# A block inversion that keeps one product and asks for its transpose two steps later, score products on 64 rows, and one modulation sum per step

## The chip, the cores and the metric

The kernel runs on one core of a Trainium2 chip. The metric is the device time of one execution in microseconds, taken as the median of several executions. Below, PE is TensorE (matrix products into PSUM banks), DVE is VectorE, ACT is ScalarE, POOL is GpSimd, and SP issues most of the DMAs. All of them run their own instructions in order and wait for each other through semaphores.

## The reference, cut to what matters

The whole kernel is two network blocks over 256 tokens of width 1024. The change lies in one stage of the first block, an RWKV-7 state recurrence with 8 heads of 64 values, and in the modulation vector that is made beside it.

```python
mod = jax.nn.silu(c) @ cond_w + cond_b          # 6 x 1024 values, one weight column per value

def step(state, inp):                            # once per token and head
    r_t, w_t, k_t, v_t, kk_t, a_t = inp
    sa = jnp.einsum('bhvk,bhk->bhv', state, -kk_t)
    state = (state * w_t[:, :, None, :]
             + sa[..., None] * (kk_t * a_t)[:, :, None, :]
             + v_t[..., None] * k_t[:, :, None, :])
    y_t = jnp.einsum('bhvk,bhk->bhv', state, r_t)
    return state, y_t
_, ys = lax.scan(step, state0, xs)
```

## The kernel before

The kernel does not step through the tokens. It cuts the 256 tokens into two chunks of 128, so that with 8 heads there are 16 pairs of chunk and head, numbered `u`. Within a pair, the effect of the tokens on each other is a strictly triangular 128 x 128 matrix of scores, and the recurrence needs the inverse of one minus that matrix. Four pairs share a PSUM bank of 512 columns and form a group `g`.

**Scores.** `amat` multiplies 128 channels of keys with 256 columns of `AR`, for one pair at a time, and DVE masks the result to a triangle (`mskb`). Two heads lie on the 128 channels. `AR` holds zeros in the 64 rows of the other head, so that the product over all 128 rows gives one head's scores. `AB` holds the scores for the inversion and `AK` those for the values.

**Inversion.** It goes by levels of doubled block size, `li` from 0 to 6. `TT` holds the inverse so far and `TN` its transpose. POOL cuts the off-diagonal blocks of a level out of `AB` into `off` (`lv_off`, one of four buffers). Level 0 sets `TT` to `off` plus one and makes `TN` from a product of `off` with the identity (`lv0`). Each later level has two parts for each group: `lvW` multiplies `off` with `TN` and lets ACT move the result into `W`; `lvD` multiplies `TT` with `W` and adds that to `TN` on DVE, and multiplies `W` with `TT` and adds that to `TT` on DVE. The 24 pairs of level (1 to 6) and group are the steps `k` of the loop over `todo`; step `k` issues `lvW` of step `k + 1` and then `lvD` of step `k`. The last level, steps 20 to 23, changes only `TT`.

**Beside the loop.** After each step `next(sd)` issues one piece of side work: the `AK` scores (`amat`), transpositions to token order (`to_tok`, and those into `RH1`), and the products of `AK` with the values (`akv`). Those take two heads' value columns for each pair, and ACT keeps the half that belongs to the head. A modulation sum (`modblk`) loads 512 KB of `cond_w` into one of three `wraw` buffers, and DVE multiplies it with `c_row` and sums along the rows (L310). It writes its products, which nobody reads, into `junk`. 24 sums stand in this stage. At one step the layer norm of the convolution branch is issued too (column sums L292 and L304, then Ln, Exp and Silu on ACT, then `ychi` and `yclo`).

**Order.** The code gives the order in which work is written, and a scheduler places the instructions on the five engines from it. Semaphores follow from who writes and reads a buffer. The weights of the next stage (`w_out`) go through the same three `wraw` buffers behind the modulation weights, and are split on ACT (L201) and DVE (L202).

Of the kernel before, what the change touches and what calls it, by code (L numbers as in the profile page):

```python
# [15 lines left out]
AF = mybir.ActivationFunctionType  # L16
# [143 lines left out]
def body(ctx: ExitStack, tc: tile.TileContext, A: dict, out: bass.AP):  # L160
# [169 lines left out]
    with ExitStack() as c1:  # L330
# [258 lines left out]
        mskb = con("msk")[:, None, :].to_broadcast([P, 2, 256])  # L589

        def amat(src, dst, u0):
            ps = bank()
            for uu in range(2):
                u = u0 + uu
                tb, h = u // 8, u % 8
                pe.matmul(ps[:, uu * T : (uu + 1) * T], src[:, h // 2, tb * P : (tb + 1) * P], AR[:, h % 2, h // 2, tb].rearrange("p a t -> p (a t)"), start=True, stop=True)
            dve.tensor_tensor(dst[:, u0 : u0 + 2].rearrange("p u a t -> p u (a t)"), r3(ps, 2), mskb, op=OP.mult)


        TT = tl([P, 16, P], "TT", "X1")  # L600
# [14 lines left out]
        def lv0(g):  # L615
            off = offs[0, g]
            dve.tensor_tensor(TT[:, gsl(g)], off, idb, op=OP.add)
            ps = bank()
            for uu in range(4):
                pe.matmul(ps[:, uu * P : (uu + 1) * P], off[:, uu], ident, start=True, stop=True)  # L620
            dve.tensor_tensor(TN[:, gsl(g)], r3(ps, 4), idb, op=OP.add)

        def lvW(li, g):
# [8 lines left out]
        def lvD(li, g):  # L632
            if li < 6:
                ps2 = bank()
                for uu in range(4):
                    pe.matmul(ps2[:, uu * P : (uu + 1) * P], TT[:, g * 4 + uu], W[:, g * 4 + uu], start=True, stop=True)
                dve.tensor_tensor(TN[:, gsl(g)], TN[:, gsl(g)], r3(ps2, 4), op=OP.add)
            ps1 = bank()
            for uu in range(4):
                pe.matmul(ps1[:, uu * P : (uu + 1) * P], W[:, g * 4 + uu], TT[:, g * 4 + uu], start=True, stop=True)  # L640
            dve.tensor_tensor(TT[:, gsl(g)], TT[:, gsl(g)], r3(ps1, 4), op=OP.add)


        vN = tl([P, 2, 512], "vN")
# [10 lines left out]
        def akv(g):  # L655
            ps = bank()
            tb = g // 2
            for uu in range(4):
                u = g * 4 + uu
                hp = (u % 8) // 2  # L660
                pe.matmul(ps[:, uu * P : (uu + 1) * P], AK[:, u, 0], vN[:, tb, hp * P : (hp + 1) * P], start=True, stop=True)
            h0 = (g % 2) * 4
            for pr in range(2):
                src = ps.rearrange("p (h r n) -> p h r n", h=2, r=4)[:, :, 3 * pr]
                if tb == 0:
                    dst = RH0[:, h0 : h0 + 4].rearrange("p (h r) n -> p h r n", r=2)[:, :, pr]
                else:
                    dst = RH1[:, h0 : h0 + 4].rearrange("p (h r) x n -> p h r x n", r=2)[:, :, pr, 1]
                act.activation(dst, src, AF.Copy)

        def side():

            for u0 in range(0, 16, 2):
                amat(ktT, AK, u0)
                yield
            for tb in range(2):
# [15 lines left out]

        for u0 in range(0, 16, 4):
            amat(bT, AB, u0)
            amat(bT, AB, u0 + 2)
            lv_off(0, u0 // 4)
        sd = side()
        for g in range(4):
# [9 lines left out]
        for k, (li, g) in enumerate(todo):  # L708
            if k + 1 < len(todo):
                lvW(*todo[k + 1])  # L710
            lvD(li, g)
            next(sd, None)
            if k % 2:
                modblk(next(mrest), c_row, junk)
            if k == 10:

                xcc, sqc = tl([P, 4, T], "xcc", "vT"), tl([P, 4, T], "sqc", "ug")
                rstdc = layer_norm(pa, yc, xcc, sqc, 4, "conv")
                ychi, yclo = tl([P, 4, T], "ychi", "yc", F32R), tl([P, 4, T], "yclo", "ug", F32R)
                for b in range(4):  # L720
                    dve.tensor_tensor(xcc[:, b], xcc[:, b], rstdc, op=OP.mult)
                    act.activation(xcc[:, b], xcc[:, b], AF.Silu, scale=col("conv_ln_g", b), bias=col("conv_ln_b", b))
                    asplit(ychi[:, b], yclo[:, b], xcc[:, b])
# [9 lines left out]
        HG = tl([P, 16, 2, 64], "HG", "X4")  # L733
        for g in range(4):
            ps = bank()
            for uu in range(4):
                u = g * 4 + uu
                h = u % 8
                if g < 2:
                    rhs = RH0[:, h - h % 2 : h - h % 2 + 2].rearrange("p a n -> p (a n)")  # L740
                else:
                    rhs = RH1[:, h].rearrange("p a n -> p (a n)")
                pe.matmul(ps[:, uu * P : (uu + 1) * P], TT[:, u], rhs, start=True, stop=True)
            if g < 2:
                for pr in range(2):
                    src = ps.rearrange("p (h r n) -> p h r n", h=2, r=4)[:, :, 3 * pr]
                    act.activation(HG[:, g * 4 : g * 4 + 4].rearrange("p (h r) x n -> p h r x n", r=2)[:, :, pr, 1], src, AF.Copy)
            else:
                act.activation(HG[:, g * 4 : g * 4 + 4].rearrange("p u a n -> p u (a n)"), r3(ps, 4), AF.Copy)


        Sb = tl([P, 4, P], "Sb", "RH0")
# [730 lines left out]
```

## Time and profile before

| what | value |
|---|---|
| median of 3 executions | 1485.28 us (1483.69 to 1488.85) |
| profiled execution, its own time | 1487.35 us |
| span from first to last instruction in it | 1485.3 us |
| PE busy / DVE busy / ACT busy | 96% / 70% / 52% of the span |
| mean granted TensorE clock | 0.989 |

The stage of the change is the stretch from about 105 to 225 us of the span, 8% of it. A time below that names a moment counts from the start of the span. PE runs a float32 product as two passes, so the trace has two records for each product, and one record for a transposition.

### The profile page before, as it was taken

What the parts mean: (1) busy time and instruction counts of PE and PEld (TensorE: products, weight loads), DVE (VectorE), ACT (ScalarE), POOL (GpSimd) and SP (SyncE); (2) the same over time, 40 slices, a digit from 0 to 9 for tenths busy, and PEclk for the clock granted to TensorE, in tenths of its full rate; (3) what the DMA queues carried; (4) which work ended last, traced back from release to release, by engine and by line L of the source; (5) the groups of instructions that cost most, each with busy time, mean ns of one, the idle gap of its engine ahead of it and who ended that gap; (6) DMA issues with size and microseconds to landing.
All of it is one profiled execution on the core that took longest, in us unless ns stands there. A gap on an engine that the chain in (4) does not pass through costs nothing.

```text
span 1485.3 us, 26041 instructions
## 1 busy us (share of the span) xinstructions
PE 1427.0 (96%) x10380; PEld 1316.3 (89%) x10381; DVE 1039.1 (70%) x1895; ACT 769.0 (52%) x1210; POOL 137.5 (9%) x96
## 2 busy tenths in 40 slices
PE   9999899799899999999999999999998999899997
PEld 6887798799899999999988888888887989799997
DVE  7779846689946777778865566655556745598886
ACT  3731436845445555444455444544446555666554
POOL 0115310134440000000000000000001000000000
PEclk9999999999999999999999999999999999999998
DMA  9676403354455555555556677766662534265552
GB/s 384 207 201 196 146 30 102 92 163 156 142 185 171 166 161 167 162 169 168 160 184 195 201 227 227 218 205 190 194 189 93 169 100 144 84 187 190 189 188 85
DMA packets 71864, 252.09 MB, mean 170 GB/s; under 512 B 7982, under 2 KB 11967, under 8 KB 70848
## 3 DMA queue, kind: packets, MB, share of 16 engines
q1 hardware_dynamic: 68990, 245.40, 52.3%
q10 hardware_dynamic: 2754, 5.05, 1.0%
q8 instruction: 81, 1.33, 0.4%
q14 instruction: 39, 0.32, 0.1%
HBM read 248.25 MB, written 2.16 MB: 169 GB/s over the span
## 4 chain that ended last, share of the span: by engine, by line
PE 82%; DVE 10%; ACT 4%; issue 2%; DMA 1%; POOL 0%; DVEq 0%; SPq 0%; ACTq 0%; POOLq 0%
PE bk L1073 23%; PE bk L213 16%; PE bk L214 16%; PE bk L216 15%; DVE junk L310 3%; PE bk L292 1%; PE bk L1005 1%; PE bk L1006 1%; PE bk L304 1%; DMA wraw<-in_cond_dram 1%; DVE wlo L202 1%; DVE eq L967 1%; ACT whi L201 1%; PE bk L640 1%; PE bk L901 1%
## 5 line engine op out<-in xcount | busy, mean ns | idle before, releaser
L201 ACT ACTIVATE whi<-wraw 128x1024 fp32r<-128x1024 f32 x400 | 423.6, 1060 | 466.3 <-PE bk L214 240.2
L202 DVE TENSOR_TENSOR wlo<-wraw,whi 128x1024 fp32r<-128x1024 f32 x376 | 462.7, 1232 | 264.8 <-ACT whi L201 256.7
L213 PE MATMUL bk<-hhi,whi 128*128 128x256 f32 x1152 | 288.5, 288 | 0.0
L214 PE MATMUL bk<-hlo,whi 128*128 128x256 f32 x1152 | 285.7, 285 | 2.2 <-DVE hlo L277 2.2
L1073 PE MATMUL bk<-whi,zs 128*128 128x512 f32 x1024 | 253.3, 390 | 1.7 <-ACT zs L276 1.7
L1073 PEld LDWEIGHTS bk<-whi,zs 128*128 128x128 f32 x1024 | 191.9, 188 | 42.3 <-ACT zs L276 1.9
L214 PEld LDWEIGHTS bk<-hlo,whi 128*128 128x128 f32 x1152 | 222.7, 193 | 2.4 <-DVE hlo L277 2.4
L213 PEld LDWEIGHTS bk<-hhi,whi 128*128 128x128 f32 x1152 | 222.7, 193 | 0.0
L216 PE MATMUL bk<-hhi,wlo 128*128 128x256 f32 x1152 | 163.1, 285 | 7.2 <-DVE wlo L202 7.0
L216 PEld LDWEIGHTS bk<-hhi,wlo 128*128 128x128 f32 x1152 | 149.6, 193 | 8.2 <-DVE wlo L202 7.8
L213 PE MATMUL bk<-hi,whi 128*128 128x256 f32 x560 | 139.6, 289 | 5.3 <-ACT hi L259 5.3
L214 PE MATMUL bk<-lo,whi 128*128 128x256 f32 x560 | 138.1, 286 | 0.1
L1073 PE MATMUL bk<-wlo,zs 128*128 128x512 f32 x512 | 136.9, 390 | 0.0
L1073 PEld LDWEIGHTS bk<-wlo,zs 128*128 128x128 f32 x512 | 96.1, 188 | 20.0
L213 PEld LDWEIGHTS bk<-hi,whi 128*128 128x128 f32 x560 | 106.5, 191 | 8.1 <-ACT hi L259 6.4
L214 PEld LDWEIGHTS bk<-lo,whi 128*128 128x128 f32 x560 | 106.5, 191 | 1.5 <-DVE lo L260 0.6
L216 PE MATMUL bk<-hi,wlo 128*128 128x256 f32 x560 | 76.7, 280 | 0.0
L202 POOL TENSOR_TENSOR wlo<-wraw,whi 128x1024 fp32r<-128x1024 f32 x24 | 63.9, 2664 | 81.2 <-ACT whi L201 81.2
L216 PEld LDWEIGHTS bk<-hi,wlo 128*128 128x128 f32 x560 | 70.4, 188 | 0.0
L1146 POOL MEMSET mq<- 64x1024 f32 x2 | 1.9, 945 | 667.2 <-PE bk L1101 667.1
L310 DVE SCALAR_TENSOR_TENSOR junk<-wraw,c_row 128x1024 bf16<-128x1024 f32 x32 | 43.8, 1368 | 23.0 <-DMA wraw<-in_cond_dram 22.9
L612 POOL TENSOR_TENSOR off<-ABt,cst 128x512 f32<-128x512 f32 x28 | 38.8, 1390 | 67.4 <-PE bk L627 51.4
(532 smaller groups left out, 2189.7 us busy)
## 6 DMA issues: line engine op xcount, KB each, us to landing
wraw<-in_u_dram SPq DMA_DIRECT2D x128, 512.0 KB, 3.6
wraw<-in_v_dram SPq DMA_DIRECT2D x128, 512.0 KB, 3.6
wraw<-in_w_up_dram SPq DMA_DIRECT2D x43, 512.0 KB, 3.6
wraw<-in_w_in_dram SPq DMA_DIRECT2D x42, 512.0 KB, 3.7
wraw<-in_cond_dram SPq DMA_DIRECT2D x32, 512.0 KB, 4.3
wraw<-in_w_down_dram SPq DMA_DIRECT2D x22, 512.0 KB, 3.8
wraw<-in_w_out_dram SPq DMA_DIRECT2D x16, 512.0 KB, 3.6
wraw<-in_wq_dram SPq DMA_DIRECT2D x16, 512.0 KB, 3.7
```

The source lines that it names most:

```text
L201: act.activation(hi, raw, AF.Copy)
L202: (sub or dve).tensor_tensor(lo, raw, hi, op=OP.subtract)
L213: pe.matmul(o, w, ahi, start=first, stop=False)
L214: pe.matmul(o, w, alo, start=False, stop=False)
L216: pe.matmul(o, wl[:, k * P : (k + 1) * P], ahi, start=False, stop=last)
L292: pe.matmul(o, lhs, x3[:, b], start=b == 0, stop=b == n - 1)
L304: pe.matmul(ps2[:, :T], ones, sq[:, b], start=b == 0, stop=b == n - 1)
L310: dve.scalar_tensor_tensor(junk, w, 1.0, c_row, op0=OP.mult, op1=OP.mult, accum_out=mod[:, b : b + 1])
L612: pool.tensor_tensor(off, AB[:, gsl(g), 0, :], lv[:, None, :].to_broadcast([P, 4, P]), op=OP.mult)
L640: pe.matmul(ps1[:, uu * P : (uu + 1) * P], W[:, g * 4 + uu], TT[:, g * 4 + uu], start=True, stop=True)
L901: pe.matmul(ps[:, (tb * 2 + half) * P : (tb * 2 + half + 1) * P], q[:, half, tb * P : (tb + 1) * P], ky[:, half], start=True, stop=True)
L1073: pe.matmul(y2[tb][half], z[:, tb * P : (tb + 1) * P], w[:, half * 512 : half * 512 + 512], start=first and k == 0, stop=last and k == 2)
```

## The change

- `amat` takes four pairs at a call. Each product uses the 64 rows of its own head; even and odd heads lie on different rows of the array and write into two banks.
- `lv0` asks for a transposition of `off` in place of a product with the identity.
- For the levels before the last, `lvD` makes the product for `TN` only. A new `lvT` transposes `TN` on PE and lets ACT copy it into `TT`. Step `k` asks for the `lvT` of step `k - 2`.
- `akv` and the first two groups of the product after the loop take the 64 columns of their own head, and ACT moves them in one instruction where it took two.
- Each step has one modulation sum; before, every second step had one and the rest stood behind the loop. In front of it ACT writes one column of `junk` from `W`, so the sum waits for that step's `W`.
- The convolution's layer norm is written at step 8, not 10.

```diff
@@ amat
-            ps = bank()
-            for uu in range(2):
+            pse, pso = bank(), bank()
+            for uu in range(4):
                 u = u0 + uu
                 tb, h = u // 8, u % 8
-                pe.matmul(ps[:, uu * T : (uu + 1) * T], src[:, h // 2, tb * P : (tb + 1) * P], AR[:, h % 2, h // 2, tb].rearrange("p a t -> p (a t)"), start=True, stop=True)
-            dve.tensor_tensor(dst[:, u0 : u0 + 2].rearrange("p u a t -> p u (a t)"), r3(ps, 2), mskb, op=OP.mult)
+                o = (pse, pso)[h % 2][:, (uu // 2) * T : (uu // 2 + 1) * T]
+                pe.matmul(o, src[hs(h), h // 2, tb * P : (tb + 1) * P], AR[hs(h), h % 2, h // 2, tb].rearrange("p a t -> p (a t)"), start=True, stop=True)
+            for r, ps in enumerate((pse, pso)):
+                d = dst[:, u0 : u0 + 4].rearrange("p (q r) a t -> p q r (a t)", r=2)[:, :, r]
+                dve.tensor_tensor(d, r3(ps, 2), mskb, op=OP.mult)
@@ lv0
-                pe.matmul(ps[:, uu * P : (uu + 1) * P], off[:, uu], ident, start=True, stop=True)
+                pe.transpose(ps[:, uu * P : (uu + 1) * P], off[:, uu], ident)
@@ lvD
                 dve.tensor_tensor(TN[:, gsl(g)], TN[:, gsl(g)], r3(ps2, 4), op=OP.add)
+                return
             ps1 = bank()
...
+        def lvT(li, g):
+            ps1 = bank()
+            for uu in range(4):
+                pe.transpose(ps1[:, uu * P : (uu + 1) * P], TN[:, g * 4 + uu], ident)
+            act.activation(TT[:, gsl(g)], r3(ps1, 4), AF.Copy)
@@ akv
-                pe.matmul(ps[:, uu * P : (uu + 1) * P], AK[:, u, 0], vN[:, tb, hp * P : (hp + 1) * P], start=True, stop=True)
+                pe.matmul(ps[:, uu * 64 : uu * 64 + 64], AK[:, u, 0], vN[:, tb, h * 64 : h * 64 + 64], start=True, stop=True)
...
@@ the loop over todo
             lvD(li, g)
+            if 2 <= k < 22:
+                lvT(*todo[k - 2])
             next(sd, None)
-            if k % 2:
-                modblk(next(mrest), c_row, junk)
-            if k == 10:
+            act.activation(junk[:, 0:1], W[:, g * 4, 0:1], AF.Copy)
+            modblk(next(mrest), c_row, junk)
+            if k == 8:
@@ the product behind the loop
+            n = 64 if g < 2 else P
...
-                pe.matmul(ps[:, uu * P : (uu + 1) * P], TT[:, u], rhs, start=True, stop=True)
+                rhs = RH0[:, h] if g < 2 else RH1[:, h].rearrange("p a n -> p (a n)")
+                pe.matmul(ps[:, uu * n : (uu + 1) * n], TT[:, u], rhs, start=True, stop=True)
```

Three places of the order show what the scheduler made of it. Lines behind the edit stand some lines later in the changed kernel, so one statement has two line numbers.

PE, around the layer norm of the convolution, before. L627 is `lvW`, L636 and L640 are the two products of `lvD`, L652 is a transposition of the side work; `cst_65` holds the identity and the ones.

```order
L627 MATMUL bk<-TN,off 128x128 x4
L636 MATMUL bk<-W,TT 128x128 x4
L640 MATMUL bk<-TT,W 128x128 x4
L652 MATMUL bk<-cst_65,X_374 128x128 x4
L292 MATMUL bk<-yc,cst_65 128x256 x4
L304 MATMUL bk<-sqc,cst_65 128x256 x4
```

The same place in the changed kernel, where L631 is `lvW`, L640 is now the one product of `lvD`, L651 is `lvT` and L692 a transposition of the side work:

```order
L631 MATMUL bk<-TN,off 128x128 x4
L640 MATMUL bk<-W,TT 128x128 x4
L651 MATMUL bk<-cst_65,TN 128x128 x4
L692 MATMUL bk<-cst_65,AR 128x128 x4
L292 MATMUL bk<-yc,cst_65 128x256 x4
L304 MATMUL bk<-sqc,cst_65 128x256 x4
```

One product of each step has become a transposition, and PE passes the layer norm two steps earlier in the loop.

DVE, at the start of the stage, before. L310 is a modulation sum, L597 a mask of `amat`, L617 and L621 the two results of `lv0`.

```order
L585 TENSOR_TENSOR bon<-bk,vT 128x512 x2
L310 SCALAR_TENSOR_TENSOR junk,mod<-wraw,c_row 128x1024
L597 TENSOR_TENSOR ABt<-bk,cst_127 128x512 x5
L617 TENSOR_TENSOR TT<-off,cst_65 128x512
L597 TENSOR_TENSOR ABt<-bk,cst_127 128x512 x3
L617 TENSOR_TENSOR TT<-off,cst_65 128x512
L621 TENSOR_TENSOR TN<-bk,cst_65 128x512
L617 TENSOR_TENSOR TT<-off,cst_65 128x512 x2
L310 SCALAR_TENSOR_TENSOR junk,mod<-wraw,c_row 128x1024 x3
L621 TENSOR_TENSOR TN<-bk,cst_65 128x512 x2
```

And in the changed kernel, where L601 is the mask and L621, L625 and L641 write `TT` and `TN`:

```order
L585 TENSOR_TENSOR bon<-bk,vT 128x512 x2
L601 TENSOR_TENSOR ABt<-bk,cst_127 128x2x256 x4
L621 TENSOR_TENSOR TT<-off,cst_65 128x512
L601 TENSOR_TENSOR ABt<-bk,cst_127 128x2x256 x2
L621 TENSOR_TENSOR TT<-off,cst_65 128x512
L601 TENSOR_TENSOR ABt<-bk,cst_127 128x2x256 x2
L625 TENSOR_TENSOR TN<-bk,cst_65 128x512
L621 TENSOR_TENSOR TT<-off,cst_65 128x512 x2
L625 TENSOR_TENSOR TN<-bk,cst_65 128x512 x3
L310 SCALAR_TENSOR_TENSOR junk,mod<-wraw,c_row 128x1024
L641 TENSOR_TENSOR TN<-TN,bk 128x512
```

The sums have moved from in front of and between the masks to a place behind all of `lv0`, and from there one stands in each step.

ACT, at the end of the loop in the changed kernel: L632 moves `W`, L721 writes the column of `junk`, L652 is the copy of `lvT`, L751 moves the product behind the loop.

```order
L632 ACTIVATE W<-bk 128x512
L721 ACTIVATE junk<-W 128x1
L201 ACTIVATE whi<-wraw 128x1024
L819 DMA memT<-in_memT_dram 128x2048
L751 ACTIVATE HG<-bk 128x4x64 x2
L751 ACTIVATE HG<-bk 128x512 x2
```

Before, the same L201 stood much earlier, in front of the layer norm:

```order
L653 ACTIVATE vN<-bk 128x512
L628 ACTIVATE W<-bk 128x512
L201 ACTIVATE whi<-wraw 128x1024
L653 ACTIVATE vN<-bk 128x512
L628 ACTIVATE W<-bk 128x512
L653 ACTIVATE bN<-bk 128x512
L299 ACTIVATE mean_conv<-bk 128x256
```

The split of the third `w_out` block has moved from the middle of the loop to its end, ahead of `HG`.

## Rows read from the trace of the kernel before

**Rows 1.** The page: busy time of the engines over the whole span.

```profile
PE 1427.0 (96%) x10380; PEld 1316.3 (89%) x10381; DVE 1039.1 (70%) x1895; ACT 769.0 (52%) x1210; POOL 137.5 (9%) x96
```

**Rows 2.** Busy time by stretch of the stage, with granted clock and DMA.

```profile
core 0: us, PE busy (x) PEld busy (x) DVE busy (x) ACT busy (x) POOL busy (x), PEclk, DMA share, GB/s
105.00:123.70 18.70, 18.63 (x193) 13.75 (x192) 15.91 (x21) 0.95 (x2) 9.77 (x7) 1.00 0.59 156
123.70:167.20 43.50, 39.84 (x319) 38.20 (x318) 42.60 (x70) 7.16 (x12) 19.85 (x13) 1.00 0.73 224
167.20:185.60 18.40, 12.76 (x83) 11.49 (x81) 12.53 (x25) 13.80 (x26) 3.69 (x4) 0.91 0.29 91
185.60:213.90 28.30, 28.29 (x252) 28.25 (x253) 11.89 (x18) 8.24 (x20) 5.45 (x5) 1.00 0.01 2
```

**Rows 3.** The chain that ended last: start, length, what, from 100 to 230 us.

```profile
104.05 4.79 DMA wraw<-in_cond_dram
108.93 1.23 DVE junk L310 x2
110.16 3.00 DVE ABt L597 x5
...
185.08 0.49 ACT W L628
185.61 1.16 PE bk L636 x8
186.77 0.89 PE bk L640 x8
187.66 0.44 PE bk L686 x4
```

**Rows 4.** Instructions in order of time: start, length, what, idle before; PE, weight loads.

```profile
105.44 7.07 PE L596 MATMUL bk<-AR,X 128*128 128x256 f32 x32
...
113.67 3.66 PE L469 MATMUL bk<-cv,wd 128*32 128x256 f32 x64
...
152.16 0.74 PEld L596 LDWEIGHTS bk<-AR,X 128*128 128x128 f32 x4
...
152.93 1.08 PEld L627 LDWEIGHTS bk<-TN,off 128*128 128x128 f32 x8
```

**Rows 5.** The same view for DVE.

```profile
105.64 0.69 DVE L585 TENSOR_TENSOR bon<-bk,vT 128x512 f32<-128x512 f32 x1 [0.17 <-PE bk L505]
...
110.08 3.08 DVE L597 TENSOR_TENSOR ABt<-bk,cst 128x512 f32<-128x512 f32 x5
```

**Rows 6.** Groups on DVE, 105 to 214 us: busy, mean ns, idle before.

```profile
L310 DVE SCALAR_TENSOR_TENSOR junk<-wraw,c_row 128x1024 bf16<-128x1024 f32 x22 | 31.5, 1433 | 3.5 <-DMA wraw<-in_cond_dram 3.4
...
L637 DVE TENSOR_TENSOR TN<-TN,bk 128x512 f32<-128x512 f32 x20 | 13.6, 682 | 16.7 <-PE bk L636 16.7
```

**Rows 7.** The same groups on ACT.

```profile
L628 ACT ACTIVATE W<-bk 128x512 f32<-128x512 f32 x24 | 14.3, 595 | 40.1 <-PE bk L627 40.1
```

**Rows 8.** The same groups on POOL.

```profile
L612 POOL TENSOR_TENSOR off<-ABt,cst 128x512 f32<-128x512 f32 x28 | 38.8, 1390 | 67.4 <-PE bk L627 51.4 <-DVE ABt L597 14.3 <-PE bk L620 1.4
```

**Rows 9.** Instructions in order of time, PE behind the loop.

```profile
219.09 0.39 PE L760 MATMUL bk<-vN,kN 128*128 128x128 f32 x2
...
219.41 1.09 PE L768 MATMUL bk<-ABt,HG 128*64 128x128 f32 x16
```

**Rows 10.** The same view around the layer norm of the convolution, all engines.

```profile
168.47 1.06 ACT L201 ACTIVATE whi<-wraw 128x1024 fp32r<-128x1024 f32 x1 [6.32 <-DMA wraw<-in_w_out_dram]
...
170.86 0.40 ACT L299 ACTIVATE mean_conv<-bk 128x256 f32<-128x256 f32 x1
...
173.01 3.05 PE L304 MATMUL bk<-sqc,cst 128*128 128x256 f32 x8 [3.83 <-ACT sqc L303]
...
175.43 1.94 PEld L627 LDWEIGHTS bk<-TN,off 128*128 128x128 f32 x8
```

**Rows 11.** The page: DMA issues, KB each, median us to landing.

```profile
wraw<-in_cond_dram SPq DMA_DIRECT2D x32, 512.0 KB, 4.3
```

More of the change, by code (lines that the diff above doesn't have):

```diff
@@ L659, in akv @@
                 u = g * 4 + uu
-                hp = (u % 8) // 2
-                pe.matmul(ps[:, uu * P : (uu + 1) * P], AK[:, u, 0], vN[:, tb, hp * P : (hp + 1) * P], start=True, stop=True)
+                h = u % 8
+                pe.matmul(ps[:, uu * 64 : uu * 64 + 64], AK[:, u, 0], vN[:, tb, h * 64 : h * 64 + 64], start=True, stop=True)
             h0 = (g % 2) * 4
[L663 to L669, printed above, removed]
+            dst = RH0[:, h0 : h0 + 4] if tb == 0 else RH1[:, h0 : h0 + 4, 1]
+            act.activation(dst, r3(ps[:, 0:256], 4), AF.Copy)
         def side():
-            for u0 in range(0, 16, 2):
+            for u0 in range(0, 16, 4):
                 amat(ktT, AK, u0)
@@ L694, in body @@
             amat(bT, AB, u0)
-            amat(bT, AB, u0 + 2)
             lv_off(0, u0 // 4)
@@ L738, in body @@
                 h = u % 8
[L739 to L742, printed above, removed]
-                pe.matmul(ps[:, uu * P : (uu + 1) * P], TT[:, u], rhs, start=True, stop=True)
[L744 to L749, printed above, removed]
+                rhs = RH0[:, h] if g < 2 else RH1[:, h].rearrange("p a n -> p (a n)")
+                pe.matmul(ps[:, uu * n : (uu + 1) * n], TT[:, u], rhs, start=True, stop=True)
+            dst = HG[:, g * 4 : g * 4 + 4, 1] if g < 2 else HG[:, g * 4 : g * 4 + 4].rearrange("p u a n -> p u (a n)")
+            act.activation(dst, r3(ps[:, 0 : 4 * n], 4), AF.Copy)
         Sb = tl([P, 4, P], "Sb", "RH0")
```

## The prediction

> **What bounds the kernel now.** I read the page first: PE is busy for 96% of the span [rows 1], so time is won where PE has less to do or waits less. The stage of the change runs from 105.0 us, when the first `AB` product starts, to 213.9 us, when the last product of the loop ends. I then asked for the busy time by stretch, cut where the limit changes [rows 2]. In the first stretch (to 123.7 us) PE shows as full. In the second (steps 0 to 10, 43.5 us) DVE is busy for 42.60 us and PE idles for 3.7 us: both are near full. In the third (18.4 us, the convolution's layer norm) PE is busy for only 12.76 us and the granted clock drops to 0.91 in the mean. In the fourth (steps 13 to 23, 28.3 us) PE is full, and DVE has half its time free.
>
> The chain of work that ended last says the same in its own way [rows 3]. It enters the stage through a DMA of modulation weights and the DVE sum behind it: the first banks of scores get their masks only from 110.1 us on, because a sum in front of them waits for that DMA. It then stays on DVE to about 170 us, goes to ACT for the layer norm, and from 185.6 us on is nothing but PE groups of 0.89 us. So a prediction has to treat the stretches apart. A product saved in the fourth is a gain in full; in the second it is a gain only if DVE is relieved too.
>
> **The prices.** A group of four products with 128 columns is 8 passes and costs 0.89 us from start to start; a group of four transpositions is 4 passes and costs 0.44 us [rows 3]. Passes with 256 columns follow each other every 0.216 us (32 in 7.07 us), so four pairs of `amat` cost 1.74 us [rows 4]. On DVE, `TN`, `TT` and mask instructions follow each other every 0.60 us (five in 3.08 us) [rows 5], and a modulation sum takes 1.43 us in the mean, more than its shortest because POOL works at the same time [rows 6]. ACT moves a bank in 0.60 us [rows 7], and POOL cuts an `off` in 1.39 us [rows 8].
>
> **The first stretch.** PE still starts at 105.0 us: the products ahead of it do not change. Two things differ. No sum stands before the masks on DVE, so the first can start when DVE has finished `bon`, at 106.3 us [rows 5], instead of 110.1. And the scores are asked for in row pairs. No row of the trace has two products of 64 rows side by side. The nearest are products that share the array by columns: passes on 64-column tiles follow each other every 0.055 us (16 in 1.09 us, less the 0.28 us that the last one lasts) where a full pass takes 0.111 [rows 9], and 32-column tiles every 0.057 us for 256 moving columns (64 in 3.66 us) where a full pass takes 0.216 [rows 4]. So the bounds are half the time and the whole time; I take half, by the 64-column row. Then `AB` ends at 108.5 us. Two masks end at 107.6, POOL has the first `off` at 109.1, its transposition ends at 109.6 (0.44, not 0.89), the first convolution (3.6 us, [rows 4]) at 113.2, two transposition groups at 114.1, the second convolution at 117.7 and the last group at 118.1. With three changes of tile shape at 0.1 us (a shape change shows 0.21 us between starts in place of 0.11 [rows 9]) the loop's first `lvW` starts at 118.5 us, against 123.7: **5.2 us**. DVE has 16 instructions of 0.6 us and more in this stretch and ends with PE.
>
> **The loop.** Five of the six levels replace a product (0.89 us) by a transposition (0.44 us), 20 times, and DVE loses 20 additions to `TT`. They come back as 20 copies on ACT. I cost the loop in four pieces.
>
> Steps 0 to 3: PE has five `lvW` and four `lvD` (8.0 us), two `lvT` (0.9 us) and four calls of `amat` at 0.87 us plus 0.2 us for two changes of shape (4.3 us): 13.2 us, to 131.7. DVE, from 119.3 us, where its last `TN` of `lv0` ends, has five sums (7.2 us), four `TN` and eight masks (7.2 us): to 133.7. DVE sets the end here, 2 us behind PE.
>
> Steps 4 to 8: PE has `lvW`, `lvD`, `lvT` and a side transposition, 2.66 us a step; DVE has a sum and a `TN`, 2.03 us. PE sets the pace: 13.3 us, to 147.0.
>
> Layer norm: before, its second sum started 3.83 us behind the first, since ACT stood still for 6.32 us on the split of a `w_out` block and made the mean only at 170.9 us [rows 10]. That split now stands behind the loop. I put 1.7 us for the first sum, 1.8 us of waiting (mean on ACT, subtraction on DVE, square on ACT: about 0.4 us each, and the way between), and 1.9 us for the second sum: 147.0 to 152.6. Then ACT works through Ln, Exp, Silu with three table loads, and `W` waits among them. Before, it took from 176.0 us (end of L304 [rows 10]) to 185.6 us (the first product that waits for that `W` [rows 3]), 9.6 us. The instructions are the same but for two copies of `lvT` in place of two other copies, so I keep 9.7 us: to 162.3. PE has 6.7 us of work to put in there and waits 3 us.
>
> The rest: 13 `lvD` and 11 `lvW` (21.4 us), 11 `lvT` (4.8 us) and three `akv` (2.7 us) make 28.9 us, to 191.2. DVE's 2.03 us a step fits beside 2.22 us, but narrowly. ACT has a `W`, a copy of `TT`, and the one column of `junk`, which no row shows; between nothing and the price of a bank it is at most 1.8 us a step. It fits at either end.
>
> `akv` and the two groups behind the loop take 64 moving columns. I give that **nothing**. Every row here with full 128-column float32 weights has at least 0.11 us between passes, whether a transposition or a product [rows 3]; the only shorter ones have narrower weights [rows 4, 9]. The other bound is half, 2.3 us less on the path. The Trainium skill says in "TensorE: Matmul & The Clock Gate", section "LDWEIGHTS (loading the stationary operand)", that loading weights takes time by their columns alone, at 1.2 columns per ns, so an estimated 107 ns for 128. By that rule the 64 columns bring nothing; by the moving columns alone the sum would be 2.3 us lower.
>
> **Sum.** The loop's end moves from 213.9 to 191.2 us: 22.7 us. Behind it the order is the same but for L201 (a rival below). The profiled execution took 1487.35 us, so 1464.7. That execution was 2.1 us above the median; counted from the median it is 1462.6. I write 1464.
>
> **The rivals.**
> - *Row pairs do not run side by side.* Then `AB` takes 7.0 us, the first `lvW` starts at 121.2, and steps 0 to 3 take 16.7 us on PE, to 137.9 in place of 133.7: 4.2 us worse, 1468. For it speaks only that no row shows them.
> - *The sums set the pace.* ACT's column of `junk` overwrites what the previous sum wrote, so it waits for that sum, and `W` stands behind it on ACT, and `lvD` behind `W`. Each sum waits for its 512 KB. With three buffers, 4.3 us to land [rows 11] and 1.43 us for the sum, one comes every 1.9 us, under the step of 2.22. The second stretch moves 224 GB/s, a load in 2.3 us, with a DMA share of 0.73 [rows 2], so there is room above that. If loads come every 2.8 us, eleven late steps lose 0.6 us and five early ones 0.1: 7 us worse, 1471.
> - *The split behind the loop.* L201 stands on ACT ahead of `HG`, and its block is loaded when the third-last sum frees a buffer, some 5.5 us before the loop ends. It lands 4.3 us later, so it just fits. A load twice as slow costs 3 us: 1467.
> - *The clock (the slower side).* While PE waited in the layer norm, the granted clock fell, and eight weight loads of `lvW` took 1.94 us [rows 10] in place of 1.08 [rows 4]: the level of 1.2 GHz. The new loop is one fifth transpositions. If PE ran at 1.2 GHz for the whole loop, its 66 us of work would double: 43 us slower than before, 1528; it decides from a third of the loop on (22.7 of 66 us). Against it: in the fourth stretch, with transpositions in its side work, the clock stays at 1.00 [rows 2]. The Trainium skill, same page, section "Part 4: PE-mode transpose", says that transpositions do not count as a busy PE in the same way; by that rule the case is worse than the fourth stretch tells, which has fewer of them; I give it little because products stand on both sides of each one.
>
> **Chances.** The forecast 0.62 (1458 to 1469, the 64 columns at half price and another microsecond or two either way), row pairs apart 0.12, sums or the split 0.19, the clock 0.03, and 0.04 that waiting I do not see takes it all back. From about 0.3% (4.5 us) on a measurement of this kernel can tell a change. All but the last two cases are faster: 0.93; same 0.03, slower 0.04. The range from 1457 to 1475 holds the forecast and the rivals up to 1471 with their own spread.
>
> **What would show it.** `lvW` first at about 118.5 us, the last product of the loop at about 191; `amat` passes every 0.11 us in pairs; `lvT` at 0.44 us a group; `akv` still 0.89 us; PE full from the layer norm to the end at 2.2 us a step; DVE waiting for PE there, not the other way. I am wrong if `W` on ACT starts late behind `junk`, if DVE is the chain through steps 12 to 22, or if the clock is under 0.95 outside the layer norm.

## The result and the profile after

The changed kernel takes 1465.33 us (median of 4 runs, 1461.16 to 1468.45) against 1485.59 us before (4 runs, 1483.69 to 1488.85). The ratio is 0.9852, with a 95% interval of 0.9832 to 0.9873: faster by 1.5%. The forecast was 1464, with a range from 1457 to 1475. The profiled execution took 1468.23 us, with a span of 1466.2 us.

The page of the changed kernel, busy time over the whole span:

```profile
PE 1411.3 (96%) x10284; PEld 1298.7 (89%) x10285; DVE 1025.5 (70%) x1875; ACT 784.1 (53%) x1248; POOL 136.5 (9%) x96
```

PE lost 15.7 us of work and DVE 13.6 us, and ACT gained 15.1 us [rows 1]. PE is still busy for 96%: the page alone does not tell where the time went, so the stage has to be cut into stretches again. Busy time by stretch, after:

```profile
105.00:118.60 13.60, 13.60 (x178) 8.70 (x177) 11.91 (x17) 0.78 (x2) 9.27 (x7) 1.00 0.27 78
118.60:132.60 14.00, 14.00 (x115) 11.93 (x113) 12.68 (x21) 5.39 (x13) 7.60 (x6) 1.00 0.50 148
132.60:146.10 13.50, 13.50 (x123) 13.50 (x122) 11.57 (x18) 8.73 (x19) 5.45 (x5) 1.00 0.62 169
146.10:160.40 14.30, 10.43 (x78) 9.48 (x76) 8.59 (x17) 12.25 (x25) 3.71 (x3) 1.00 0.21 66
160.40:191.10 30.70, 30.70 (x260) 30.70 (x261) 25.46 (x39) 17.88 (x42) 9.79 (x7) 0.94 0.69 209
```

PE is full in four of the five stretches, and the only waits are 3.87 us in the layer norm. Before, PE idled for 3.7 us in steps 0 to 10, while DVE was busy for 42.60 of 43.5 us, and for 5.6 us in the layer norm [rows 2]. The DMA traffic is spread too: 148, 169, 66 and 209 GB/s in the loop, where it ran at 224 GB/s to the layer norm and at 2 GB/s behind it.

The chain that ended last, after:

```profile
105.76 3.65 PE bk L598 x32
109.41 0.61 PE bk L624 x4
...
118.82 1.79 PE bk L631 x16
...
132.63 1.09 PE bk L631 x8
...
146.13 1.74 PE bk L292 x8
...
149.24 1.99 PE bk L304 x8
151.23 0.91 PE bk L631 x8
...
160.39 2.08 PE bk L640 x8
162.47 0.85 PE bk L651 x4
163.32 1.14 PE bk L672 x8
164.46 0.95 PE bk L631 x8
165.41 0.89 PE bk L640 x8
166.30 0.44 PE bk L651 x4
166.74 0.84 PE bk L672 x8
...
191.28 3.57 PE bk L749 x32
```

The chain that ran over DMA, DVE and ACT before [rows 3] now stays on PE from 105.76 us to the layer norm, passes through ACT there, and comes back at 160.39 us. Line by line: 32 score passes in 3.65 us (L598), `lvW` (L631), `lvD` (L640), `lvT` at 0.44 us a group (L651), `akv` at 0.84 us (L672). The first product behind the loop (L749, L743 before) starts at 191.28 us in place of 214.12. That is 22.8 us. I use this moment, "the loop's end", in all the experiments, because the rest of the program is noisier than the stage: from the loop's end to the end of the span the profiles take 1271.2 us before and 1274.9 after, and between 1267.3 and 1277.1 us in the runs below, which share that code but for the first two product groups. So the 22.8 us show as 19.1 in the two spans and as 20.3 in the two medians.

### The profile page after: what moved, and what is told of

It is laid out like the page before. It is cut to its first block, busy times and chain, and to the rows that moved or that the text cites. A ratio compares the mean times of both kernels' runs of the same rounds, so it can differ in the third digit from the quotient of the medians.

```text
span 1466.2 us, 25857 instructions
## 1 busy us (share of the span) xinstructions
PE 1411.3 (96%) x10284; PEld 1298.7 (89%) x10285; DVE 1025.5 (70%) x1875; ACT 784.1 (53%) x1248; POOL 136.5 (9%) x96
## 4 chain that ended last, share of the span: by engine, by line
PE 81%; DVE 8%; ACT 5%; DMA 4%; issue 1%; POOL 0%; DVEq 0%; ACTq 0%; SPq 0%; POOLq 0%
PE bk L1075 18%; PE bk L213 16%; PE bk L214 16%; PE bk L216 16%; DMA wraw<-in_v_dram 2%; DMA wraw<-in_cond_dram 2%; DVE wlo L202 2%; PE bk L292 1%; ACT whi L201 1%; PE bk L631 1%; PE bk L640 1%; PE bk L1007 1%; DVE junk L310 1%; PE bk L1008 1%; PE bk L469 1%
## 5 line engine op out<-in xcount | busy, mean ns | idle before, releaser
L201 ACT ACTIVATE whi<-wraw 128x1024 fp32r<-128x1024 f32 x400 | 423.5, 1060 | 463.9 <-PE bk L214 238.6
L310 DVE SCALAR_TENSOR_TENSOR junk<-wraw,c_row 128x1024 bf16<-128x1024 f32 x32 | 42.0, 1312 | 24.8 <-DMA wraw<-in_cond_dram 17.1
L214 PE MATMUL bk<-fl,whi 128*128 128x256 f32 x176 | 42.6, 280 | 0.0
```

The costliest lines, as they stand in the source:

```text
L201: act.activation(hi, raw, AF.Copy)
L214: pe.matmul(o, w, alo, start=False, stop=False)
L310: dve.scalar_tensor_tensor(junk, w, 1.0, c_row, op0=OP.mult, op1=OP.mult, accum_out=mod[:, b : b + 1])
```

## The experiments

The change has three parts that could carry the gain: **the column** (ACT writes one column of `junk` ahead of each modulation sum, and the sums are asked for once a step), **the pairs** (scores on 64 rows) and **the transpositions** (those of level 0, and `lvT` two steps behind). Two smaller parts go along with them: the 64 moving columns (experiment 8), and the layer norm's move from step 10 to step 8, which no run tests by itself. My theory was that the gain is a sum over parts: so much PE time from the pairs and the transpositions, some DVE time from the sums. The rival was that one part does nearly all, or that they only work together.

**1. The transpositions alone**, on the kernel before (level 0 transposes too; the cut below shows only the loop).

```diff
+                return
...
+            if 2 <= k < 22:
+                lvT(*todo[k - 2])
```

> The kernel before, with the transpositions of the change alone (level 0, and one for each step two steps behind); scores, sums and columns as before. My sum, stretch by stretch: the sum ahead of the masks stays, so the first lvW starts only 0.9 to 1.4 us earlier (about 122.5 us); steps 0 to 10 stay on DVE, which loses about ten additions of 0.60 us, so 5.5 to 6 us; the later steps lose 0.45 us each. The loop ends at about 203.5 us instead of 213.9, 10 us less in all, about 1475. Rival, the sums on DVE take it back: steps 0 to 10 as long as before, the loop ends at 208 to 209 us, about 5 us less. Rival, the transpositions carry nearly the whole gain: 195 us or earlier.

Measured: 1479.34 us against 1488.36, ratio 0.9947 (0.9930 to 0.9964); loop's end at 209.44 us. That is 4.7 us, so the first rival held. Of these, 2.0 us come from level 0, ahead of the loop: the first `lvW` starts at 121.8 us in place of 123.8. PE loses 20 x 0.45 = 9 us of work in the loop, and only 2.7 us of them show. DVE with its sums is busy for 38.04 of 40.7 us from the first `lvW` to the layer norm, and PE's waits in the stage grow from 9.3 to 12.9 us. The granted clock behind the layer norm is 0.94 here, where it was 1.00; that takes another 1.6 us.

**2. The changed kernel without the column.**

```diff
-            act.activation(junk[:, 0:1], W[:, g * 4, 0:1], AF.Copy)
```

> The changed kernel without the column of junk that ACT writes; the scheduler is free to put the sums where it likes, and puts nearly all ahead of the layer norm. My theory: the gate is worth much, since a sum ahead of the masks waits for its DMA (first lvW at about 121.8 us, not 118.6), and 22 sums of 1.4 us with nine TN and eight masks keep DVE busy until about 156 us, so that the layer norm's second column sum starts at 156 to 157 us instead of 149.2. The loop ends at about 199 us instead of 191.3, 7 to 8 us more, about 1473. Rival, the gate does nothing because PE has the longer steps anyway: the loop ends at 191 to 192 us, 1465.

Measured: 1482.53 us, ratio 0.9961 (0.9946 to 0.9975); loop's end at 210.34 us. One column of 128 elements, which nobody reads, is worth 19.1 us of the 22.8. I had expected 7 to 8 us. Its busy time by stretch, and then DVE and ACT ahead of the layer norm:

```profile
122.90:157.20 34.30, 30.73 (x235) 27.40 (x234) 33.44 (x53) 11.89 (x22) 16.74 (x11) 0.95 0.77 234
157.20:169.80 12.60, 5.08 (x18) 3.90 (x17) 8.78 (x16) 4.64 (x9) 0.31 (x1) 0.73 0.79 245
169.80:210.10 40.30, 37.75 (x322) 37.49 (x321) 14.20 (x22) 24.10 (x44) 11.45 (x10) 0.96 0.02 9
```

```profile
157.48 1.23 DVE L310 SCALAR_TENSOR_TENSOR junk<-wraw,c_row 128x1024 bf16<-128x1024 f32 x1 [0.91 <-DMA wraw<-in_cond_dram]
...
161.47 1.23 DVE L310 SCALAR_TENSOR_TENSOR junk<-wraw,c_row 128x1024 bf16<-128x1024 f32 x1 [1.02 <-DMA wraw<-in_cond_dram]
...
163.50 1.22 DVE L310 SCALAR_TENSOR_TENSOR junk<-wraw,c_row 128x1024 bf16<-128x1024 f32 x1 [0.19 <-DMA wraw<-in_cond_dram]
...
164.85 1.42 DVE L302 TENSOR_TENSOR xcc<-yc,mean_conv 128x256 f32<-128x256 f32 x4
165.19 1.06 ACT L201 ACTIVATE whi<-wraw 128x1024 fp32r<-128x1024 f32 x1 [5.68 <-DMA wraw<-in_w_out_dram]
```

Without the column a sum depends on nothing but its load, so DVE's program has them early: the last of the 24 starts at 163.50 us, and the layer norm's subtraction stands behind all of them, at 164.85. PE has finished the first column sum at 159 us by then and idles for 7.5 us of 12.6, at a granted clock of 0.73; the second starts at 166.6 us, where I had expected 156 to 157. The split L201 stands there too: ACT waits 5.68 us for its block, which is loaded behind the sums' blocks in the same three buffers, and can square the first difference only at 166.16 us. Without the column L201 is in front of these squares in every run (before, experiments 1, 2 and 6), and with the column it stands at the end of the loop; no run holds back the sums and leaves the split in front. Of the 19.1 us, 11.2 lie ahead of the first column sum and 7.8 in the layer norm; in both a part is the lower clock. With the column each sum follows a `W`, and the last one starts at 190.33 us. So "one sum per step" in the text of the loop is not what spreads them. The column is.

**3. The changed kernel with 128 rows in the scores.**

```diff
-src[hs(h), h // 2, tb * P : (tb + 1) * P], AR[hs(h), h % 2, h // 2, tb]
+src[:, h // 2, tb * P : (tb + 1) * P], AR[:, h % 2, h // 2, tb]
```

> The changed kernel with score products over all 128 rows, still two banks and four pairs at a call. My theory, row pairs share the array: AB takes 7.0 us instead of 3.7 and AK 1.74 us a call instead of 1.06. The first lvW starts 2.5 to 3 us later and steps 0 to 3 take 2 to 2.7 us longer; the loop ends at about 196.5 us instead of 191.3, about 1470. Rival, the masks on DVE would hide it: 1 us or less, the loop ends at 192.

Measured: 1467.48 us, ratio 0.9862 (0.9841 to 0.9884); loop's end at 196.06 us, 4.8 us later, as the theory said. From its chain:

```profile
105.60 6.91 PE bk L598 x32
...
121.73 1.79 PE bk L631 x16
```

The 32 passes of `AB` take 6.91 us in place of 3.65: 0.216 and 0.114 us a pass, so row pairs do lie side by side. `AB` gives 2.9 us (first `lvW` at 121.73), the four calls in the loop 1.9.

**4. The column alone**, on the kernel before.

```diff
-            if k % 2:
-                modblk(next(mrest), c_row, junk)
+            act.activation(junk[:, 0:1], W[:, g * 4, 0:1], AF.Copy)
+            modblk(next(mrest), c_row, junk)
```

> The kernel before with ACT's one column of junk and one sum per step alone: products of the doubling, scores on 128 rows and the layer norm at step 10 as before. Left out of the changed kernel: transpositions, row pairs, 64 columns. Theory (the order of the sums was DVE's part of the limit, the products are PE's): masks no longer stand behind sums, first lvW at about 121 us in place of 123.7; a step costs PE 2.67 us with its products (3.6 with a side group) and DVE 1.36 + 1.2 us, so PE sets the pace and is full outside the layer norm; the loop ends at 202 to 205 us, 9 to 12 us below before, 1475 to 1478. Rival 1: the order is everything, as the 19 us that the changed kernel loses without it say: loop's end at 195 or below, 1469 or less. Rival 2: without lighter products the order brings nothing: end at 210 or above.

Measured: 1479.77 us, ratio 0.9939 (0.9919 to 0.9959); loop's end at 206.56 us: 7.6 us, a little short of the theory's 9 to 12. Its chain is PE from 105.64 us to 164.1, the end of the first column sum: the products, not DVE, set the pace now. Busy time from the first `lvW` to the layer norm, and behind it:

```profile
123.70:162.30 38.60, 38.60 (x317) 37.78 (x317) 34.83 (x54) 10.82 (x26) 15.06 (x13) 1.00 0.52 150
...
177.90:206.50 28.60, 28.60 (x245) 28.60 (x245) 23.30 (x38) 9.59 (x28) 5.46 (x5) 0.95 0.58 168
```

The first `lvW` stands at 123.69 us as before, not at the 121 that I had expected: the 128-row scores, the products of level 0 and the convolutions fill PE for that long anyway. Behind the layer norm the clock of 0.95 costs some 1.4 us.

**5. The changed kernel without the transpositions of the loop** (products on `TT` put back; level 0 still transposes).

```diff
-                return
...
-            if 2 <= k < 22:
-                lvT(*todo[k - 2])
```

> The changed kernel with the products of the doubling on TT put back (five levels, 20 groups of 0.89 us and an addition on DVE each) in place of the transpositions; ACT's column and one sum a step, row pairs and 64 columns kept. Alone, on the kernel before, the transpositions brought 4.7 us at the loop's end. Theory (they bring their whole 20 x 0.45 us of PE, and more through DVE's 20 additions, once the sums are spread): steps cost DVE 0.68 + 0.68 + 1.4 = 2.76 us and PE 2.67, the loop ends at 201 to 206 us in place of 191.3, time 1475 to 1479. Rival (the sums and row pairs did it, transpositions bring 5 us here too): loop's end at 196, 1470.

Measured: 1470.49 us, ratio 0.9886 (0.9859 to 0.9912); loop's end at 197.52 us. The transpositions bring 6.2 us here, nearer to the rival's 5 than to the theory's 10 to 15.

```profile
150.00:170.00 20.00, 17.44 (x139) 16.48 (x138) 15.03 (x27) 13.59 (x29) 4.52 (x5) 1.00 0.26 83
170.00:196.00 26.00, 26.00 (x235) 26.00 (x235) 24.80 (x41) 8.48 (x22) 6.83 (x7) 1.00 0.63 201
```

Their 20 x 0.45 = 9 us of PE time are there. But in the layer norm the heavier loop has more to put into the wait (PE idles for 2.56 us in place of 3.87, 1.3 us), and this execution did not have the fall of the clock that cost the changed kernel some 1.7 us there (last section). 9 - 1.3 - 1.7 = 6.0.

**6. The pairs alone**, on the kernel before (the `amat` of the change, called for four pairs at a time as there).

```diff
-                pe.matmul(ps[:, uu * T : (uu + 1) * T], src[:, h // 2, tb * P : (tb + 1) * P], AR[:, h % 2, h // 2, tb]
+                pe.matmul(o, src[hs(h), h // 2, tb * P : (tb + 1) * P], AR[hs(h), h % 2, h // 2, tb]
```

> The kernel before with the score products on 64 rows alone, in pairs that share the array; products in the doubling, the sums' place and 128 moving columns as before. It saves PE 7 us of passes. Theory (without ACT's column DVE, with the sums in front of masks and TN, sets the pace to the layer norm, and what PE saves there turns into waits; with transpositions but without the column the pairs brought nothing): loop's end at 212 to 214.5 us, 0 to 2 us below before, ratio 0.998 to 1.001. Rival (the pairs' passes lie on the path as they do with the column in place, 4.8 us): loop's end at 209.3, 1483.

Measured: 1485.40 us against 1486.21, ratio 0.9989 (0.9976 to 1.0002); loop's end at 214.94 us, 0.8 later than before and 0.4 above the range. But for that the theory held: PE's saved time turns into waits. In the first stretch PE shows it, busy for 9.62 of 13 us (the granted clock is 0.87 there, and the first `lvW` starts at 125.7 us, where it was 123.8):

```profile
105.00:118.00 13.00, 9.62 (x90) 6.23 (x92) 10.17 (x16) 0.00 (x0) 5.66 (x5) 0.87 0.81 210
118.00:165.00 47.00, 43.12 (x396) 37.31 (x388) 46.76 (x69) 9.31 (x16) 19.44 (x14) 1.00 0.62 197
```

DVE is busy for 46.76 of the next 47 us. With this the three parts make a table of the loop's end (us):

| | neither | pairs | transpositions | both |
|---|---|---|---|---|
| without the column | 214.12 (before) | 214.94 | 209.44 | 210.34 |
| with the column | 206.56 | 197.52 | 196.06 | 191.28 (after) |

Without the column the pairs are worth nothing (-0.8, -0.9); with it 4.8 us beside the transpositions. Between 206.56 and 197.52 lie 9.0 us, but these are not the pairs alone: the run of experiment 5 also keeps the transpositions of level 0 (2.0 us, the first `lvW` of experiment 4 against that of experiment 3) and did not have the fall of the clock (1.4 us in experiment 4). That leaves some 5.6 us, near the 4.8. All runs of the lower row but 206.56, and 210.34 in the upper, also have the layer norm at step 8 and the 64 moving columns; experiment 8 prices the columns at nothing, and for the layer norm's place no run has a price.

Clean of all this is the column against the rest of the change (the asking for a sum in every step counts with the column in experiment 4 and with the rest in experiment 2). The rest without the column brings 3.8 us (experiment 2), the column without the rest 7.6 us (experiment 4), and 11.4 of the 22.8 us come only when both are there. My theory of a sum over parts falls: PE's savings count only where DVE with its sums, and ACT with the split behind their loads, no longer set the pace.

**7. The transposition in the step of its own products**, then one step behind, then in its own step without sums.

```diff
-            if 2 <= k < 22:
-                lvT(*todo[k - 2])
+            if k < 20:
+                lvT(li, g)
```

> The changed kernel with lvT asked for in the step of its own products, so PE meets it directly behind lvD of that group, whose TN DVE must add first. Theory: the transposition waits for lvD's end and the addition (about 0.6 us and the way to DVE and back, 1 us in all), behind it nothing else of PE runs unless the scheduler puts the next lvW in between; 20 steps at about 1 us, less where the side work fills: loop's end at 203 to 211 us in place of 191, 1477 to 1487. Rival: the scheduler orders by readiness anyway or the wait is filled by lvW of the next group: under 3 us.

Measured: 1510.32 us, ratio 1.0138 (1.0121 to 1.0155): slower than the kernel before; loop's end at 239.64 us, 48.4 us later, where I had expected 12 to 20. One late step in order of time:

```profile
212.13 0.66 PE L651 MATMUL bk<-cst,TN 128*128 128x128 f32 x4 [1.27 <-DVE TN L641]
...
212.63 1.06 PE L631 MATMUL bk<-TN,off 128*128 128x128 f32 x8
...
213.72 0.60 ACT L632 ACTIVATE W<-bk 128x512 f32<-128x512 f32 x1 [0.30 <-PE bk L631]
...
214.35 0.21 ACT L721 ACTIVATE junk<-W 128x1 bf16<-128x1 f32 x1
214.59 1.41 DVE L310 SCALAR_TENSOR_TENSOR junk<-wraw,c_row 128x1024 bf16<-128x1024 f32 x1 [2.51 <-ACT junk L721]
...
215.93 0.68 DVE L641 TENSOR_TENSOR TN<-TN,bk 128x512 f32<-128x512 f32 x1
...
216.66 0.66 PE L651 MATMUL bk<-cst,TN 128*128 128x128 f32 x4 [2.09 <-DVE TN L641]
```

Read the releasers from the bottom: `lvT` waits for `TN` on DVE; `TN` stands behind a sum; the sum waited for ACT's column; the column for `W`; `W` for `lvW`; and `lvW` stands on PE behind the previous `lvT`. That is a ring of 4.53 us a step, where PE has 2.2 us of work. The whole loop, PE's waits for `TN` (us in all, times, the longest):

```profile
PE bk L651 <- DVE TN L641: 33.5, 20, 2.1
```

The rest of the 48.4 us is mostly the granted clock: it is down in all three stretches of this loop, so that PE's own work takes some 17 us longer than in the changed kernel (85.7 us busy from the first `lvW` to the loop's end, where it was 68.6):

```profile
118.80:174.30 55.50, 38.41 (x241) 33.50 (x241) 25.82 (x40) 15.66 (x33) 12.91 (x11) 0.84 0.31 88
174.30:190.00 15.70, 12.34 (x77) 10.53 (x75) 7.01 (x16) 12.07 (x25) 3.20 (x2) 0.91 0.18 58
190.00:239.60 49.60, 34.91 (x254) 33.11 (x255) 23.56 (x37) 17.48 (x41) 9.28 (x8) 0.90 0.41 119
```

Then the same without the sums:

```diff
-            modblk(next(mrest), c_row, junk)
+            dve.memset(mod[:, 16 + k : 17 + k], 0.5)
+            next(mrest)
```

> Leaves out the 24 modulation sums and their loads (mod is filled with a constant, so the time stands for the loop alone), lvT in the step of its products. With the sums, lvT there ended the loop at 239.6 us. Theory (the sum between ACT's column and TN is what makes the ring slow): without it PE waits only for lvD's end and TN, 0.7 to 1.0 us a step, and the loop ends at 203 to 210 us. Rival (the wait for TN itself costs the 48 us): 230 or above.

Measured (one run): loop's end at 209.12 us, a late step of 3.22 us, and in the same view of waits:

```profile
PE bk L651 <- DVE TN L641: 15.6, 20, 0.8
```

So the theory held: the wait for `TN` itself costs 0.78 us a step, and the sum that the column puts into the ring turns a step of 3.22 us into one of 4.53. The clock stays at 1.00 in this loop, and PE is busy for 71.2 us, so that the waits lengthen PE's own work by only 2.6 of the 17 us above. The delay and the column belong together: with the column but without the delay, the kernel is slower than before the change.

And one step behind:

```diff
-            if 2 <= k < 22:
-                lvT(*todo[k - 2])
+            if 1 <= k < 21:
+                lvT(*todo[k - 1])
```

> The changed kernel with lvT one step behind its products in place of two. Theory (in the step's own place lvT closed a ring lvW, W on ACT, junk column, sum, TN, lvT of 4.5 us a step; one step behind, TN of the step before is ready after lvW and lvD, 1.8 us, less than the 2.3 us that the sum and TN need behind lvD's start): a small wait of up to 0.5 us a step stays in the late steps, loop's end at 191 to 200 us, 1465 to 1473. Rival: the ring stays, one step longer, and a step takes 3 us or more: loop's end at 210 or above, 1484.

Measured: 1463.84 us, ratio 0.9844 (0.9822 to 0.9866); loop's end at 190.32 us. PE waits for `TN` once, for 0.4 us. One step of delay opens the ring; the second brings nothing that shows.

**8. 128 moving columns in `akv` and behind the loop**, the rest as changed.

```diff
-                pe.matmul(ps[:, uu * 64 : uu * 64 + 64], AK[:, u, 0], vN[:, tb, h * 64 : h * 64 + 64], start=True, stop=True)
+                pe.matmul(ps[:, uu * P : (uu + 1) * P], AK[:, u, 0], vN[:, tb, hp * P : (hp + 1) * P], start=True, stop=True)
```

> The changed kernel with 128 moving columns in akv and in the first two groups behind the loop, as before the change (ACT again moves them in two pieces). Theory (a pass of full float32 weights costs 0.11 us whatever the moving columns): akv 0.89 in place of 0.84 us, loop's end 0 to 0.5 us later, time within 0.2% of the changed kernel. Rival: moving columns count by half: 2.3 us later, 1467.5.

Measured: 1464.62 us, ratio 0.9833 (0.9816 to 0.9851), against 0.9852 for the changed kernel: no difference. A group of `akv` takes 0.89 us, with 64 columns 0.84:

```profile
161.91 0.89 PE bk L672 x8
```

**9. The layer norm in pieces** (column sums at steps 6 and 8, Silu at 10, one `ychi` block at each of steps 11 to 14), on the changed kernel; then with two `junk` tiles in turn.

```diff
-            if k == 8:
+            if k == 6:
...
+                colsum(ps[:, :T], ones, yc, 4)
...
+            if k == 8:
...
+                colsum(ps2[:, :T], ones, sqc, 4)
...
+            if 11 <= k < 15:
+                b = k - 11
+                asplit(ychi[:, b], yclo[:, b], xcc[:, b])
```

> The changed kernel with the convolution's layer norm written in pieces: first column sum, mean and squares at step 6, second column sum, Ln and Exp at step 8, Silu at step 10, the splits one at each of steps 11 to 14. My theory, what is left of waiting in the loop (1.4 us before the second column sum, 2.5 us for W behind Silu, and 1.7 us of the lower clock after that) comes only from the order: PE does not wait there, the clock stays up, and the loop ends at about 186 us instead of 191.3, about 1460. Rival, ACT's work (three table loads, some 13 us beside the copies) only moves its delay: W waits elsewhere, the loop ends at 189 to 191 us.

Measured: 1462.54 us, ratio 0.9824 (0.9801 to 0.9848); loop's end at 188.2 us, 3.1 us earlier than in the changed kernel, where I had expected 5.3. PE's wait before the second column sum is gone, 1.6 us of waiting for `W` are left of 2.5, and the clock is 1.00 throughout. But the chain in the last 13 us is now this:

```profile
175.53 1.44 DVE junk L310 x2
...
176.99 5.82 DMA wraw<-in_cond_dram
...
182.90 1.25 DVE junk L310 x2
...
184.16 4.58 DMA wraw<-in_cond_dram
...
188.83 1.24 DVE junk L310 x2
```

The sums and their loads end last. That is the rival of the prediction, "the sums set the pace", which turns up as soon as PE is 3 us faster.

```diff
-            act.activation(junk[:, 0:1], W[:, g * 4, 0:1], AF.Copy)
-            modblk(next(mrest), c_row, junk)
+            act.activation(junks[k % 2][:, 0:1], W[:, g * 4, 0:1], AF.Copy)
+            modblk(next(mrest), c_row, junks[k % 2])
```

> The kernel with the layer norm in pieces, with two junk tiles in turn: ACT's column in step k waits for the sum of step k - 2, not k - 1. Theory (late in that loop ACT, and with it W and lvD, stands behind the sum of the step before, 14.9 us of the waits between 118 and 190 us): those waits go, HG starts at 184 to 186 us in place of 188.2, 1458 to 1460. Rival: the sums themselves, 24 at 1.36 us and their loads of 512 KB, set the pace, so the wait only moves from ACT to DVE or the DMA: HG at 188 and no change of the time.

Measured: 1462.43 us, ratio 0.9827 (0.9807 to 0.9847); loop's end at 186.50 us, so 1.7 us from the second tile, between the theory's 184 to 186 and the rival's 188, and nothing more in the time. The intervals of both versions overlap that of the changed kernel; I don't call them faster.

## Why the prediction was right

The time and the loop's end (191.2 forecast, 191.28 measured) agree, but some terms were off and cancelled: measured less forecast, the pieces below were off by +0.3, -1.4, +0.2, -0.5, -0.5 and +2.0 us. The agreement to 0.1 us is luck. That PE sets the pace outside the layer norm came out as forecast, but for steps 0 to 3, where I had named DVE.

- **First stretch.** `amat` in pairs by the 64-column row [rows 9]: 3.5 us forecast, 3.65 measured. First `lvW` 118.5, measured 118.82. Right, and the rival of row pairs apart is out (experiment 3).
- **Steps 0 to 3.** I wrote "DVE sets the end here, 2 us behind PE", at 133.7. PE went on at 132.63. DVE did finish late, at 134.36, but its last work there is a pair of masks for `AK`, and PE needs those only in `akv`, 20 us later. Counting an engine's busy time as the end of a piece is wrong where the next piece waits for only part of it. PE's own time was 0.6 us longer than my 13.2, since an `lvW` behind `amat` costs 1.09 us, not 0.89. Net 1.4 us too long.
- **Steps 4 to 8.** 13.3 us, measured 13.5. Right.
- **Layer norm.** 5.6 us, measured 5.1 (1.74, a wait of 1.38, 1.99). My three terms (1.7, 1.8 and 1.9) add up to 5.4 and not to the 5.6 that I carried on. ACT's chain 9.7 us, measured 9.16. Each half a microsecond too long.
- **The rest.** 28.9 us, measured 30.89: 2.0 too short. The step takes 2.2 us as forecast; the first groups behind ACT's chain take 2.08, 0.85 and 1.14 us in place of 1.16, 0.44 and 0.84, because the clock was down. That is 1.6 us, the same kind of fall to the lower level that stood in [rows 10], which I had read but had not charged. The other 0.4 us: the first group behind a wait takes 1.16 us (also in [rows 3]) where I charged 0.89, and an `lvW` behind an `akv` 0.95.
- **64 columns: nothing.** 0.84 us a group, as against a bound of half. The Trainium skill ("TensorE: Matmul & The Clock Gate", section "LDWEIGHTS (loading the stationary operand)") gives weights an estimated 107 ns for 128 columns. The trace agrees in the distance from one pass to the next, 105 ns (8 in 0.84 us); the record of a single load lasts longer, 192 ns.
- **The clock rival.** The granted clock is 1.00 from 105 to 160.4 us and again from 165 us on, with `lvT` in nearly every step. Over the whole last stretch it is 0.94, just under the 0.95 that I had named as a sign of being wrong; the 4.6 us behind the layer norm, at 0.63, make that mean, and on both sides of them the clock is 1.00 with the same transpositions. By the Trainium skill, same page, section "Part 4: PE-mode transpose", it might have fallen; at this share of transpositions the traces do not show it (1.00 in all stretches of experiment 9).
- **The sums rival.** In the changed kernel PE's waits in the loop are 1.4 us for the layer norm and 2.5 us for `W` behind it; DVE waits for the column 7.4 us and for loads 0.5 us, and none of it reaches PE. The split of L201 is not on the chain either.
- **What makes the order.** The sum was right because I had taken the order of the sums and of the split from the changed program. I priced what that order gives (masks that wait for no sum, an earlier second column sum, DVE beside PE), but I did not ask what makes it: ACT's column stands in the prediction only as a cost, "at most 1.8 us a step" with the `W` and the copy, and as the start of a rival. The runs show that the order hangs on this column: without it the rest of the change brings 3.8 us of the 22.8. I undervalued it after the result too: experiment 2 was expected to lose 7 to 8 us and lost 19.

The gain at the loop's end (22.8) is larger than the one between medians (20.3); the unchanged code behind it takes up the rest. I did not find out what in it varies.

## What to carry to other kernels

When two engines are both near full, saved work on one can be worth next to nothing until the other is relieved (here -0.8 us for the pairs alone), so test each part with and without the others before crediting it. Where a scheduler sets the order, a line's place in the loop does not hold work back; a cheap false dependency does, but draw the ring that it can close before placing it. Asking for the consumer one step behind its producer broke such a ring here; a second step was not needed.

## What was not expected of the hardware

The clock's fall behind the layer norm does not follow from PE's waits alone. The changed kernel and the one of experiment 8 have the same waits there (PE busy for 10.53 and 10.52 of 14.4 us), and yet the next 4.6 us ran at 0.63 and at 1.00. After:

```profile
146.00:160.40 14.40, 10.53 (x79) 9.58 (x77) 8.69 (x17) 12.35 (x25) 3.71 (x3) 1.00 0.21 68
160.40:165.00 4.60, 4.60 (x26) 4.60 (x27) 1.92 (x3) 2.33 (x7) 0.00 (x0) 0.63 0.33 85
```

With 128 columns (experiment 8):

```profile
146.00:160.40 14.40, 10.52 (x78) 9.57 (x76) 8.60 (x17) 12.35 (x25) 3.72 (x3) 1.00 0.21 66
160.40:165.00 4.60, 4.60 (x42) 4.60 (x43) 3.52 (x6) 3.10 (x11) 1.16 (x1) 1.00 0.29 82
```

PE got 26 matmuls done in those 4.6 us in the one and 42 in the other, which is why experiment 8's loop ends 1.7 us earlier (189.56) without any gain of its own. Just behind the layer norm the clock fell in experiments 1, 3 and 4 as well, and not in 5, 7 (one step behind) and 8. Each of these is one execution; whether another execution of the same kernel would do the same is not shown. In experiment 7 it stayed at 1.00 with waits of 0.78 us in 20 steps (without sums), and was 0.84, 0.91 and 0.90 with waits of up to 2.1 us in 20 steps.
